# A list scheduler gets TensorE durations per pair of instructions, and puts a wide matmul between two fp32 transposes

## The chip, the cores and the metric

The kernel runs on one core of a Trainium2 chip. The metric is the device time of one execution in microseconds (us). The engines that matter are TensorE (PE in the profile; PEld is its weight load), VectorE (DVE), ScalarE (ACT), GpSimd (POOL) and SyncE (SP), whose queue issues the loads from memory.

## The reference

Two transformer blocks of two layers each run one after the other on 512 tokens of 1024 channels, all in fp32. Cut to what is computed:

```
# block 1
x = x + diff_attention(rms_norm(x))             # 8 heads, two causal softmaxes per head, a = p0 - lam * p1
x = x + swiglu(rms_norm(x))                     # hidden width 2816
x = x + swa_sink_attention(rms_norm(x))         # 16 query heads, 4 key heads, window 128, a sink per head
x = x + swiglu(rms_norm(x))
# block 2, with a second stream xc of 256 context tokens and shifts and gates from silu(c) @ w_mod
x  = x  + g1 * conv_mixers(modulate(rmsnorm(x)))     # depthwise convolutions of 3 and 31 taps
xc = xc + cg1 * conv_mixers(modulate(rmsnorm(xc)))
x, xc = each + gate * conv_ffn(modulate(rmsnorm(.))) # hidden width 2816, a convolution of 3 taps
x = x + g1 * windowed_gqa(x, xc)                     # 128-token blocks, three blocks and the context as keys
x = x + g2 * conv_ffn(modulate(rmsnorm(x)))
return rmsnorm(x, final_norm)
```

## The kernel before

Activations lie with channels on the 128 partitions and tokens along the free axis, so the stream is 8 tiles of 128 x 512. Every fp32 product is made of three products in float32r: a value is split into a rounded part and a remainder, and `mm3` (L727) issues high x high, high x low and low x high into the same PSUM bank. A product's stationary operand has 128 columns, its moving operand 512 or 256 (half of the tokens, or the context), 384 or 128 in the attentions.

Four other kinds of instruction run on PE. Their names in the profile's rows are the tiles that they read:

- an fp32 transpose of 128 x 128 (`psum_t<-arenaF`, 128x128). Attention transposes the softmax's weights, up to four blocks in a row (L1204 and L1585); `bcast` (L690) makes a column of one factor per token into a row for all partitions, as the last step of a norm; the end of the kernel turns its output (L1843). There are 566.
- a float32r transpose of 128 x 128 (`psum_t<-arenaR`, 128x128), four in a row per token block of queries and keys (L984). There are 296.
- an fp32 product with a single column of ones (`psum_t<-arenaF`, 128x1), which sums squares over the partitions (`colsum_rsqrt`, L677). There are 80, and the trace has two records for each.
- narrow float32r products of 128 columns, 112 of them, in rows like those of the float32r transposes.

A norm of a stage is a chain through three engines: the squares' sums (128x1) on PE, Ln and Exp on ScalarE, a Newton step on VectorE, `bcast` on PE, and then the scaled tiles on VectorE and ScalarE, which the next products read. Attention has a chain of its own for every block of queries: scores on PE, mask, maximum and exponential on VectorE and ScalarE, transposes on PE, the split on ScalarE and VectorE, then the products with the values.

**What sets the order.** The kernel's functions don't issue instructions: they record them. `Rec.add` (L275) notes for each its dependences and a cost in ns (`cost`, L314). When a stage is recorded, `issue` (L343) sets the order in seven rounds of list scheduling: `forward` (L393) gives each engine, whenever it is free, the ready instruction with the lowest priority number; `backward` (L455) runs the same from the end and returns for each instruction the latest start that does not lengthen the schedule, which is the priority number of the next round. The shortest of the schedules is issued, and so is fixed for every engine. A copy may go to ScalarE or VectorE (`flex`, L269), whichever the schedule finds free. The numbers for PE are per instruction:

```python
            if fn == "transpose":
                return 59 if dt == F32R else 109
            if dt == F32:
                return max(n * 1.685, 214)
            if dt == F32R:
                return max(n * 0.4222, 107)
```

so 216 ns for 512 columns and 108 for 256, and an engine is free again when the cost has passed. The functions that the diff touches follow.

Of the kernel before, what the change touches and what calls it, by code (L numbers as in the profile page):

```python
# [19 lines left out]
S = 512  # L20
# [12 lines left out]
ROUNDS = 7  # L33
WO1_AT = (2, 3, 5, 7)
# [20 lines left out]
# ---------------------------------------------------------------- column map of the parameter table  # L55
# [125 lines left out]
# ---------------------------------------------------------------- recorded program  # L181
# Instructions are recorded in program order and issued in an order that a list scheduler finds: every
# instruction stays behind those that it depends on (data, or reuse of the same on-chip memory).
# [4 lines left out]
# the activation functions whose tables are not in every set; ln and exp can be had together  # L188
# [12 lines left out]
class Rec:  # L201
    ENG = ("tensor", "vector", "scalar", "gpsimd", "sync")

    def __init__(self, nc, psum):
# [13 lines left out]
        self.free = {e: 0.0 for e in self.ENG}  # L218
        self.dma = 0.0
# [3 lines left out]
    # regions as keys  # L223
# [45 lines left out]
    def flex(self, first, second):  # L269
        """(engine, function, args, kwargs) twice: the same work on either engine, the first preferred"""  # L270
        eng, fn, a, k = second
        o, i = self.add(*first, flex=True)
        self.alt[len(self.ops) - 1] = (eng, fn, a, k, self.cost(eng, fn, a, k, o, i))

    def add(self, eng, fn, a, k, flex=False):  # L275
# [9 lines left out]
        for x in ins:  # L285
            for key in self.keys(x):
# [4 lines left out]
                if key[0] == "p":  # L291
                    # two engines never read a bank at the same time
# [11 lines left out]
        self.ops.append((eng, fn, a, k, deps, self.cost(eng, fn, a, k, outs, ins), i + self.bias))  # L304
        return outs, ins
# [8 lines left out]
    def cost(self, eng, fn, a, k, outs, ins):  # L314
# [3 lines left out]
        if eng == "tensor":  # L318
            dt = (k.get("rhs") if fn == "matmul" else a[1]).dtype
            if fn == "transpose":  # L320
                return 59 if dt == F32R else 109
            if dt == F32:
                return max(n * 1.685, 214)
            if dt == F32R:
                return max(n * 0.4222, 107)
            return max(n * 0.4222, 29)
# [16 lines left out]
    def issue(self, until=None):  # L343
        """order and issue what was recorded and not issued yet, or only as much as it takes to issue the set `until`"""
# [17 lines left out]
        # priorities: the order of the program at first, then the latest starts that leave the schedule as short as it is  # L362
# [13 lines left out]
        order, eng, fin, self.free, self.dma = self.forward(todo, succ, pred, at, prio, wanted)  # L376
# [12 lines left out]
    def lat(e, e2):  # L389
        """from the end of an instruction to the start of one that waits for it"""  # L390
        return (0 if e == "tensor" else 260) if e2 == "tensor" else (197 if e == "tensor" else 130)

    def forward(self, todo, succ, pred, at, prio, wanted=None):  # L393
# [1512 lines left out]
```

## Time and profile before

| | us |
|---|---|
| median of 3 runs (lowest to highest) | 2588.99 (2587.46 to 2589.8) |
| the profiled execution: span from the first to the last instruction, all that is recorded of its time | 2587.4 |
| PE busy | 2554.9 |
| VectorE busy | 1873.2 |
| ScalarE busy | 1252.5 |
| PE waiting for another engine, in gaps over 0.15 us | 25.6 |

In the profile a matmul's duration runs from its start to its modelled end, and several overlap; how far apart two starts are tells the pace. The timeline merges instructions that follow each other on one line with the same tiles into one row, which shows the start of the first, the time to the end of the last, the first one's shape and the count. A stretch that is cut to a few ns begins with the instruction that is then running, and so shows one instruction's start.

### The profile page before, as it was taken

Reading aid. Unit: us, or ns where it says so; the run is one execution under the profiler, and the core shown is the slowest. Engines: PE = TensorE matmul, PEld = TensorE weight load, DVE = VectorE, ACT = ScalarE, POOL = GpSimd, SP = SyncE. Lnnn points to the kernel's source line nnn. Section 1 sums busy time; section 2 is a strip of 40 time slices with the busy share of each in tenths; the row PEclk is TensorE's granted clock in tenths of the full one; section 3 lists DMA queues with packets and bytes.
Section 4 is the critical chain, followed back from the end, with each engine's and each line's share of the span. In section 5 each row is a group of like instructions: output and inputs, shape, how many; then the busy total and the mean of one; then the engine's idle time right before and its main releaser. Section 6 shows DMA issues by size and latency. Waiting matters only on the chain.

```text
span 2587.4 us, 38865 instructions
## 1 busy us (share of the span) xinstructions
PE 2554.9 (99%) x15122; PEld 2263.3 (87%) x15122; DVE 1873.2 (72%) x3499; ACT 1252.5 (48%) x2361; POOL 131.0 (5%) x252
## 2 busy tenths in 40 slices
PE   8999999999999999999999999999999999999998
PEld 8998988889979888889888988888889988888887
DVE  8888999845898999449986753454556899864555
ACT  6876522224896322336664431231335798532333
POOL 0000000000010000004830000000000000000000
PEclk9999999999999999999999999999999999999999
DMA  4122567632125676322122112122112111333332
GB/s 147 57 62 71 188 211 220 180 95 78 58 66 155 203 223 195 120 90 66 58 66 62 58 58 73 58 62 70 58 58 63 50 34 42 98 98 98 94 99 69
DMA packets 73337, 252.80 MB, mean 98 GB/s; under 512 B 8513, under 2 KB 10689, under 8 KB 72769
## 3 DMA queue, kind: packets, MB, share of 16 engines
q1 hardware_dynamic: 73152, 250.32, 31.9%
q8 instruction: 118, 1.93, 0.3%
q14 instruction: 67, 0.54, 0.1%
HBM read 248.19 MB, written 2.10 MB: 97 GB/s over the span
## 4 chain that ended last, share of the span: by engine, by line
PE 93%; DVE 3%; POOL 2%; ACT 2%; issue 1%; DMA 0%; DVEq 0%; POOLq 0%; SPq 0%; ACTq 0%
PE psum_t L384 93%; POOL arenaZ L384 2%; DVE arenaR L384 1%; DVE arenaF L384 1%; ACT arenaF L384 1%; ACT arenaR L384 1%; DMA arenaF<-in_wqkv_dram 0%; DMA arenaF<-in_xT_dram 0%; ACT L382 0%; ACT L384 0%; DVE psum_t L384 0%; ACT arenaZ L384 0%; DVEq L1902 0%; DVE arenaZ L384 0%; POOLq L384 0%
## 5 line engine op out<-in xcount | busy, mean ns | idle before, releaser
L384 PE MATMUL psum_t<-arenaR 128*128 128x256 f32 (+2 forms) x13304 | 2374.1, 337 | 13.1 <-ACT arenaR L384 7.9
L384 PEld LDWEIGHTS psum_t<-arenaR 128*128 128x128 f32 x13304 | 2050.0, 188 | 280.0 <-ACT arenaR L384 9.0
L384 ACT CAST arenaR<-arenaF 128x1024 fp32r<-128x1024 f32 (+4 forms) x500 | 447.9, 899 | 816.5 <-PE psum_t L384 622.5
L384 DVE TENSOR_TENSOR arenaR<-arenaF,arenaR 128x1024 fp32r<-128x1024 f32 (+3 forms) x508 | 529.4, 1049 | 154.2 <-ACT arenaR L384 150.5
L384 ACT ACTIVATE arenaF<-arenaF 128x256 f32<-128x256 f32 (+9 forms) x776 | 405.9, 542 | 236.5 <-DVE arenaF L384 201.1
L384 DVE SCALAR_TENSOR_TENSOR arenaF<-psum_t,arenaF 128x511 f32<-128x511 f32 (+5 forms) x416 | 262.7, 634 | 287.2 <-PE psum_t L384 163.5
L384 DVE CUSTOM_DVE_ANT_0 arenaF<-arenaF 128x1024 f32<-128x1024 f32 x192 | 246.0, 1281 | 10.0 <-DMA arenaF<-in_wmod_dram 4.6
L384 DVE TENSOR_TENSOR arenaF<-arenaF 128x512 f32<-128x512 f32 (+5 forms) x430 | 220.6, 525 | 27.6 <-ACT arenaF L384 21.8
L384 DVE TENSOR_TENSOR arenaF<-psum_t,arenaF 128x512 f32<-128x512 f32 (+1 forms) x236 | 142.5, 611 | 134.9 <-PE psum_t L384 133.9
L384 PE MATMUL psum_t<-arenaZ,arenaR 128*128 128x256 f32 (+3 forms) x1024 | 178.1, 304 | 2.3 <-DVE arenaF L384 1.4
L384 ACT CAST arenaR<-psum_t 128x512 fp32r<-128x512 f32 (+3 forms) x332 | 157.2, 480 | 28.7 <-PE psum_t L384 25.7
L384 ACT ACTIVATE arenaF<-psum_t,arenaF 128x512 f32<-128x512 f32 (+3 forms) x204 | 109.0, 548 | 111.4 <-PE psum_t L384 103.6
L384 PEld LDWEIGHTS psum_t<-arenaZ,arenaR 128*128 128x128 f32 x1024 | 145.5, 189 | 12.8 <-DVE arenaF L384 2.7
L384 POOL TENSOR_TENSOR arenaZ<-arenaZ,arenaF 128x256 f32<-128x256 f32 x120 | 104.3, 870 | 446.7 <-DVE arenaF L384 423.6
L384 PE MATMUL psum_t<-arenaF 128*128 128x128 f32 (+2 forms) x730 | 114.2, 268 | 9.5 <-DVE arenaF L384 4.1
L384 DVE CUSTOM_DVE_ANT_0 arenaF<-psum_t,arenaF 128x256 f32<-128x256 f32 (+3 forms) x208 | 103.8, 512 | 14.3 <-PE psum_t L384 13.2
L384 PEld LDWEIGHTS psum_t<-arenaF 128*128 128x128 f32 x730 | 89.5, 152 | 21.3 <-DVE arenaR L384 4.9
L384 DVE TENSOR_TENSOR arenaR<-psum_t,arenaR 128x512 fp32r<-128x512 f32 (+4 forms) x169 | 99.1, 591 | 12.2 <-ACT arenaR L384 10.8
L384 POOL COPY arenaF<-arenaF 128x1 f32<-128x1 f32 x128 | 26.5, 234 | 1599.1 <-DVE arenaF L384 1172.7
L384 ACT ACTIVATE arenaR<-arenaF 128x256 fp32r<-128x256 f32 (+1 forms) x168 | 81.7, 525 | 32.3 <-DVE arenaF L384 24.4
L384 DVE SCALAR_TENSOR_TENSOR arenaR<-arenaF,arenaR 128x256 fp32r<-128x256 f32 (+1 forms) x168 | 79.5, 505 | 8.0 <-ACT arenaR L384 7.7
L384 DVE SCALAR_TENSOR_TENSOR arenaF<-arenaF 128x256 f32<-128x256 f32 (+8 forms) x258 | 79.9, 332 | 3.5 <-ACT arenaF L384 1.9
(47 smaller groups left out, 450.2 us busy)
## 6 DMA issues: line engine op xcount, KB each, us to landing
arenaF<-in_wmod_dram SPq DMA_DIRECT2D x96, 512.0 KB, 4.3
arenaF<-in_wgu_dram SPq DMA_DIRECT2D x88, 512.0 KB, 3.8
arenaF<-in_wup_dram SPq DMA_DIRECT2D x88, 512.0 KB, 3.6
arenaF<-in_wqkv_dram SPq DMA_DIRECT2D x35, 512.0 KB, 3.7
arenaF<-in_wd_dram SPq DMA_DIRECT2D x32, 448.0 KB, 3.3
arenaF<-in_wdn_dram SPq DMA_DIRECT2D x32, 448.0 KB, 3.3
arenaF<-in_wab_dram SPq DMA_DIRECT2D x20, 512.0 KB, 3.6
arenaF<-in_wd_dram SPq DMA_DIRECT2D x16, 512.0 KB, 4.3
```

What stands on the lines that cost most here:

```text
L384: getattr(getattr(self.nc, e), fn)(*a, **k)
```

## The change

The scheduler's model of PE changes, and nothing that is computed. The costs of an instruction become n / 2.4 + 13.3 ns for float32r products (227 for 512 columns, 120 for 256), 85 for a float32r transpose, and at least 224 for an fp32 product. Each PE instruction gets a kind: F for fp32, S for float32r transposes and products under 256 columns, L for wide float32r products. How long one holds PE depends on the next (`hold`): an fp32 transpose 109 ns before another F, 28 ns before anything else; S before S 62 ns; all others their cost. Its result still comes after its cost. `forward` keeps a second heap, `between`, of the ready L instructions. Where the next instruction would be an F behind an F, the ready L of the lowest priority number is taken first, if its number is less than SLACK = 4000 ns above that of the F. `backward` uses 48 ns for an fp32 transpose and 62 for S. All comments and docstrings are taken out too, which shifts the line of the issuing call from L384 to L387.

```diff
+SLACK = 4000
...
+        self.kinds = {}
+        self.pe = None
...
+        if eng == "tensor":
+            self.kinds[i] = self.kind(i)
...
             if fn == "transpose":
-                return 59 if dt == F32R else 109
+                return 85 if dt == F32R else 109
             if dt == F32:
-                return max(n * 1.685, 214)
-            if dt == F32R:
-                return max(n * 0.4222, 107)
-            return max(n * 0.4222, 29)
+                return max(n * 2 / 1.2, 224)
+            return max(n / 2.4 + 13.3, 110)
...
+    def kind(self, i):
+        _, fn, a, k = self.ops[i][:4]
+        if (k.get("rhs") if fn == "matmul" else a[1]).dtype == F32:
+            return "F"
+        return "S" if fn == "transpose" or self.fsize(a[0]) < 256 else "L"
+
+    def hold(self, i, j):
+        fn, c = self.ops[i][1], self.ops[i][5]
+        x, y = self.kinds[i], self.kinds[j]
+        if x == "F" and fn == "transpose":
+            return 109 if y == "F" else 28
+        return 62 if x == y == "S" else c
...
     def forward(self, todo, succ, pred, at, prio, wanted=None):
...
+        between = []
...
                     heapq.heappush(ready[e], (prio[i] + (e != ops[i][0]) * 10000, i))
+                    if e == "tensor" and kinds[i] == "L":
+                        heapq.heappush(between, (prio[i], i))
             _, i = heapq.heappop(ready[e])
+            if e == "tensor":
+                while between and between[0][1] in took:
+                    heapq.heappop(between)
+                if kinds[i] == "F" and pe is not None and kinds[pe[0]] == "F" and between and between[0][0] < prio[i] + SLACK:
+                    heapq.heappush(ready[e], (prio[i], i))
+                    _, i = heapq.heappop(between)
+                if pe is not None:
+                    t = max(t, pe[1] + self.hold(pe[0], i))
+                pe = i, t
...
+            elif e == "tensor":
+                fin[i] = t + c
+                free[e] = t + (28 if kinds[i] == "F" else 62 if kinds[i] == "S" else c)
             else:
                 free[e] = fin[i] = t + c
...
     def backward(self, todo, succ, pred, took, fin):
...
+            elif e == "tensor":
+                done = t + c
+                free[e] = t + (48 if self.kinds[i] == "F" and ops[i][1] == "transpose" else 62 if self.kinds[i] == "S" else c)
```

The change moves instructions on PE nearly everywhere outside the feed-forward layers. Three places follow, each with PE's rows before and then now.

**Place A**, PE, a head of the first attention (the trace of before has it from 104.5 us on). `arenaF 128x128` are the four fp32 transposes of a query block's weights, `arenaR 128x256` and `128x384` products. Before:

```order
L384 MATMUL psum_t<-arenaF 128x128
L384 MATMUL psum_t<-arenaR 128x256 x12
L384 MATMUL psum_t<-arenaF 128x128 x4
L384 MATMUL psum_t<-arenaR 128x256 x8
L384 MATMUL psum_t<-arenaR 128x384 x2
```

Now:

```order
L387 MATMUL psum_t<-arenaR 128x384 x2
L387 MATMUL psum_t<-arenaR 128x256
L387 MATMUL psum_t<-arenaF 128x128
L387 MATMUL psum_t<-arenaR 128x256
L387 MATMUL psum_t<-arenaF 128x128
L387 MATMUL psum_t<-arenaR 128x256
L387 MATMUL psum_t<-arenaF 128x128
L387 MATMUL psum_t<-arenaR 128x256
L387 MATMUL psum_t<-arenaF 128x128
L387 MATMUL psum_t<-arenaR 128x256 x11
```

The same four transposes now have a product of 256 columns between each two of them.

**Place B**, PE, the same attention some 7 us earlier (98.5 us in the trace of before). `arenaR 128x128 x4` are the four float32r transposes of a block of queries and keys, `arenaF 128x128` fp32 transposes. Before:

```order
L384 MATMUL psum_t<-arenaR 128x256 x15
L384 MATMUL psum_t<-arenaF 128x128 x4
L384 MATMUL psum_t<-arenaR 128x256 x12
L384 MATMUL psum_t<-arenaR 128x128 x4
L384 MATMUL psum_t<-arenaR 128x256 x12
```

Now:

```order
L387 MATMUL psum_t<-arenaR 128x256 x10
L387 MATMUL psum_t<-arenaR 128x128
L387 MATMUL psum_t<-arenaR 128x256
L387 MATMUL psum_t<-arenaR 128x128
L387 MATMUL psum_t<-arenaR 128x256
L387 MATMUL psum_t<-arenaR 128x128
L387 MATMUL psum_t<-arenaR 128x256
L387 MATMUL psum_t<-arenaF 128x128
L387 MATMUL psum_t<-arenaR 128x128
L387 MATMUL psum_t<-arenaR 128x256
```

The four float32r transposes are taken apart too, by products and by an fp32 transpose.

**Place C**, PE, the end of the second block's attention (2198.9 us on in the trace of before), where a norm begins. `arenaF 128x1` are that norm's column sums, the last `arenaF 128x128 x2` before is its `bcast`, `arenaR,arenaZ 128x512` are products with the values. Before:

```order
L384 MATMUL psum_t<-arenaF 128x128 x4
L384 MATMUL psum_t<-arenaR,arenaZ_11793 128x512 x2
L384 MATMUL psum_t<-arenaR 128x512
L384 MATMUL psum_t<-arenaR 128x256 x2
L384 MATMUL psum_t<-arenaR 128x512 x2
L384 MATMUL psum_t<-arenaR 128x256 x4
L384 MATMUL psum_t<-arenaR 128x512
L384 MATMUL psum_t<-arenaR 128x256
L384 MATMUL psum_t<-arenaF 128x1 x2
L384 MATMUL psum_t<-arenaR 128x256 x18
L384 MATMUL psum_t<-arenaF 128x128 x2
L384 MATMUL psum_t<-arenaR 128x256 x130
```

Now:

```order
L387 MATMUL psum_t<-arenaF 128x128
L387 MATMUL psum_t<-arenaR,arenaZ_11792 128x512
L387 MATMUL psum_t<-arenaF 128x128 x5
L387 MATMUL psum_t<-arenaR 128x512
L387 MATMUL psum_t<-arenaF 128x1
L387 MATMUL psum_t<-arenaR 128x512
L387 MATMUL psum_t<-arenaF 128x1
L387 MATMUL psum_t<-arenaR 128x512 x2
L387 MATMUL psum_t<-arenaF 128x128
L387 MATMUL psum_t<-arenaR 128x256
L387 MATMUL psum_t<-arenaF 128x128
L387 MATMUL psum_t<-arenaR 128x256 x114
```

The 18 products that stood between the sums and the `bcast` now stand behind it; products that stood ahead of the sums stand between them.

## Rows read from the trace of the kernel before

**Rows 1.** The page's busy times with shares, and PE's granted clock by slices.

```profile
PE 2554.9 (99%) x15122; PEld 2263.3 (87%) x15122; DVE 1873.2 (72%) x3499; ACT 1252.5 (48%) x2361; POOL 131.0 (5%) x252
...
PEclk9999999999999999999999999999999999999999
```

**Rows 2.** The page's chain that ended last, share by engine.

```profile
PE 93%; DVE 3%; POOL 2%; ACT 2%; issue 1%; DMA 0%; DVEq 0%; POOLq 0%; SPq 0%; ACTq 0%
```

**Rows 3.** PE's waits by releaser: us in total, times, longest.

```profile
PE psum_t L384 <- ACT arenaR L384: 7.9, 4, 6.5
PE psum_t L384 <- DVE arenaR L384: 7.7, 12, 1.8
PE psum_t L384 <- DVE arenaF L384: 7.2, 10, 2.4
PE psum_t L384 <- ACT arenaZ L384: 2.5, 2, 1.6
PE psum_t L384 <- ACT arenaF L384: 0.3, 1, 0.3
```

**Rows 4.** PE's timeline, two long runs: start us, us, line, operation, shape, xcount.

```profile
309.81 30.54 PE L384 MATMUL psum_t<-arenaR 128*128 128x512 f32 x134
...
29.84 10.36 PE L384 MATMUL psum_t<-arenaR 128*128 128x256 f32 x85
```

**Rows 5.** PE's timeline around place A, cut to show single starts.

```profile
104.50 0.27 PE L384 MATMUL psum_t<-arenaF 128*128 128x128 f32 x1
104.53 1.68 PE L384 MATMUL psum_t<-arenaR 128*128 128x256 f32 x12
...
105.92 0.28 PE L384 MATMUL psum_t<-arenaR 128*128 128x256 f32 x1
...
106.04 0.60 PE L384 MATMUL psum_t<-arenaF 128*128 128x128 f32 x4
106.39 2.25 PE L384 MATMUL psum_t<-arenaR 128*128 128x256 f32 x16
...
106.60 0.40 PE L384 MATMUL psum_t<-arenaR 128*128 128x256 f32 x2
```

**Rows 6.** PE's timeline, fp32 transposes among products of 512 columns.

```profile
2138.03 0.60 PE L384 MATMUL psum_t<-arenaF 128*128 128x128 f32 x4
...
2138.70 0.27 PE L384 MATMUL psum_t<-arenaF 128*128 128x128 f32 x1
2138.73 0.94 PE L384 MATMUL psum_t<-arenaR 128*128 128x512 f32 x3
...
2139.04 0.39 PE L384 MATMUL psum_t<-arenaR 128*128 128x512 f32 x1
```

**Rows 7.** PE's timeline, float32r transposes: four at place B, one elsewhere.

```profile
98.48 0.45 PE L384 MATMUL psum_t<-arenaR 128*128 128x128 f32 x4
...
98.97 0.40 PE L384 MATMUL psum_t<-arenaR 128*128 128x256 f32 x2
...
664.93 0.39 PE L384 MATMUL psum_t<-arenaR 128*128 128x128 f32 x2
...
665.16 0.40 PE L384 MATMUL psum_t<-arenaR 128*128 128x256 f32 x2
```

**Rows 8.** PE's timeline at a norm; in brackets idle before, and releaser.

```profile
1956.35 0.61 PE L384 MATMUL psum_t<-arenaF 128*128 128x1 f32 x4
1956.82 1.91 PE L384 MATMUL psum_t<-arenaR 128*128 128x256 f32 x14
1959.66 0.43 PE L384 MATMUL psum_t<-arenaF 128*128 128x128 f32 x2 [0.93 <-DVE arenaF L384]
```

**Rows 9.** PE's timeline, stalls in block 2's attention and at place C.

```profile
2111.54 0.66 PE L384 MATMUL psum_t<-arenaF 128*128 128x128 f32 x4 [1.85 <-DVE arenaR L384]
...
2204.22 1.45 PE L384 MATMUL psum_t<-arenaR 128*128 128x256 f32 x10 [1.25 <-DVE arenaR L384]
2206.20 0.38 PE L384 MATMUL psum_t<-arenaR 128*128 128x256 f32 x1 [0.54 <-DVE arenaF L384]
```

More of the change, by code (lines that the diff above doesn't have):

```diff
@@ L375, in issue @@
                 prio = best[1]
-        order, eng, fin, self.free, self.dma = self.forward(todo, succ, pred, at, prio, wanted)
+        order, eng, fin, self.free, self.dma, self.pe = self.forward(todo, succ, pred, at, prio, wanted)
         for i in order:
@@ L391, in lat @@
         return (0 if e == "tensor" else 260) if e2 == "tensor" else (197 if e == "tensor" else 130)
+    def kind(self, i):
[9 more added lines that the diff above has]
+        return 62 if x == y == "S" else c
     def forward(self, todo, succ, pred, at, prio, wanted=None):
-        ops, alt, lat = self.ops, self.alt, self.lat
-        free, dma = dict(self.free), self.dma
+        ops, alt, lat, kinds = self.ops, self.alt, self.lat, self.kinds
+        free, dma, pe = dict(self.free), self.dma, self.pe
+        between = []
         left = {i: len(pred[i]) for i in todo}
@@ L452, in forward @@
                     push(s)
-        return order, took, fin, free, dma
+        return order, took, fin, free, dma, pe
     def backward(self, todo, succ, pred, took, fin):
```

## The prediction

> **What bounds the kernel now.** I read the page's busy line and clock line first: the reader is to see TensorE (PE) busy for 99% of the span, VectorE 72%, ScalarE 48%, and a clock line with no slice below nine tenths [rows 1]. Then the chain of work that ended last: 93% of it is PE's own instructions following each other [rows 2]. Then PE's waits by releaser: 25.6 us in all (7.9 + 7.7 + 7.2 + 2.5 + 0.3) [rows 3]. The longest of them, 6.5 us, is the wait for the first operands, which no reordering touches, so 19.1 us of stalls are left. Everything else is the pace at which PE starts one instruction after the other. So the change can act in two ways only: through that pace, and through those 19.1 us. DMA ends none of PE's waits [rows 3], so the moved issues on SP's queue cost nothing; what hides them is that the weights wait in their buffers.
>
> A matmul's listed duration is pipelined and says little about pace, so I read starts. 134 products of 512 columns last from 309.81 to 340.35 [rows 4], and a lone one at 2139.04 is 0.39 long [rows 6]: (30.54 - 0.39) / 133 = 0.227 us from start to start. 85 of 256 columns take 10.36 us [rows 4], one at 105.92 is 0.28 long [rows 5]: (10.36 - 0.28) / 84 = 0.120 us.
>
> **The premise: 28 ns after a transpose.** The new table says that an fp32 transpose holds PE 109 ns before another fp32 instruction, but 28 ns before a wide product. Both numbers stand in the trace. Four transposes start at 106.04 and the product behind them at 106.39: 0.35 = 3 x 0.109 + 0.028. A single one starts at 104.50, its product at 104.53 [rows 5]. But the next row has the bill. After the four, the first product of 256 columns holds PE from 106.39 to 106.60, 0.20 us in place of 0.120. So four transposes cost 106.60 - 106.04 - 0.12 = 0.44 us, 0.11 each. The single one: from 104.50 to 106.04 there are one transpose and 12 products; 1.54 - 12 x 0.120 = 0.10 us. A transpose costs 0.10 to 0.11 us whether it stands alone or in four: 81 ns saved at its own start are lost in the following product. Beside products of 512 columns it is the same: four and their product take 2138.70 - 2138.03 = 0.67, less 0.227 leaves 0.44, 0.11 each; a single one and its product 2139.04 - 2138.70 = 0.34 us against 0.109 + 0.227 = 0.336 [rows 6].
>
> The Trainium skill speaks against the change here: "TensorE: Matmul & The Clock Gate", section "LDWEIGHTS (loading the stationary operand)", has a load take its columns divided by 1.2, 107 ns for 128, so a short transpose cannot cover the load of what follows it. The rows agree: 0.028 + 0.08 makes 0.108. By that rule the transposes' term is 0; by the new table it is -24.8 us, the first rival below. The same page, section "The mechanism", lets a load overlap running matmuls only where they use other rows of the array. Here all use all 128, and that would put 0.107 us ahead of every product; the row of 85 products has 0.120 us for load and product together, so loads do hide behind a product and the measurement decides. By that section interleaving would be free everywhere, 0 for the next term too; the sum would then be 4.1 us less.
>
> **The change part by part.** The same 15,040 PE instructions are issued; counted in the two orders, neighbours of two fp32 transposes fall from 384 to 78, so 306 are split.
>
> - fp32 transposes before 256 columns (160 of the 306): 0, by the price above. Before 512 (96): 4 ns each, 0.4 us. The other 50 stand before products of 384 or 128 columns or float32r transposes, taken as 0. Bounds: 0 to 2 us.
> - float32r transposes. The new rule is only about fp32, but products pulled forward also land between these: runs rise from 80 to 257 (place B). Four in a row start at 98.48, the second product behind them at 98.97: 0.49 - 0.12 = 0.37 us. One alone starts at 664.93, the second product behind it at 665.16: 0.23 - 0.12 = 0.11 us [rows 7]. So each added run costs (4 x 0.11 - 0.37) / 3 = 0.023 us more: 177 x 0.023 = 4.1 us. A hundredth either way in the starts gives the bounds: 0.10 alone makes 0.01, 0.12 alone 0.037, so 2 and 7 us; 0 if the delay of the product is absorbed where it stands before 512 columns.
> - fp32 column sums of one column: 49 neighbours fall to 0, and none stands alone in the trace. Two take 1956.82 - 1956.35 = 0.47 us [rows 8]. If alone they cost what a transpose does, 0.11 in place of 0.235, it is -6 us; if they pay the float32r step, +1 us. I take 0: two passes mean two loads, which the nearest row prices alike in any company.
> - 20 copies move from ScalarE to VectorE (the scheduler's own choice), 33 in place of 13. VectorE is busy 72% of the span [rows 1], so some 0.6 us each lies beside PE's work, and costs only where PE waits for VectorE, which is in the next term.
> - Stalls. In the model PE now runs through transposes 81 ns too fast, and the rule takes products early that used to stand where PE waits for a chain. Place C shows it: the column sums of a norm are followed in the old order by 18 products before the norm's broadcast, in the new one by two of 512, 0.45 us. What that chain takes is seen at another norm, where PE did wait for it: from 1956.82, behind the sums, to the broadcast at 1959.66, 2.84 us [rows 8]. So PE idles some 2.84 - 0.45 = 2.4 us there, where it now idles 1.25 + 0.54 = 1.79 [rows 9]: +0.6 us. Queued behind the waiting broadcast are the 114 products that would have covered it, and the rest of the norm on VectorE waits for it. Over the whole program I counted, at the paces above, the PE work between the last PE instruction that a wait goes back to and the instruction that waits: under 1.0 us in 26 places before, in 52 now. If stalls followed that count they would double, +19 us; on the other side, ahead of the transposes that now wait 1.85 us at 2111.54 [rows 9] the same count gives 3.2 us of work in place of 1.4, and if half of today's stalls dissolved in that way it would be -10 us. I take +5, a quarter of the doubling, since most of the short covers sit in the same few places, where one wait absorbs the next.
>
> Sum: 0.4 + 4.1 + 0 + 5 = 9.5 us on the profiled execution's 2587.4: 2596.9. The runs' median of 2588.99 lies 1.6 above that execution, so 2598.5; I say 2598. Its own range, with the pace at 0 to 9 and the stalls at 0 to 10: 2589 to 2608.
>
> **Rivals.**
> 1. The 28 ns are real wherever transpose and product alternate: 306 x 0.081 = 24.8 us gained, less the 4.1: 2589 - 20.7 = 2568. For it: the starts behind the transposes [rows 5]. Against it: the start after the next in the same rows, and the single transpose among products of 512 columns [rows 6]. Chance 0.04.
> 2. Not slower, by fewer stalls: the table's wide products are now 120 and 227 ns, as the trace has them [rows 4], where the old formula gave 108 and 216, so the planner sees how long PE covers a chain and places consumers later. The place is the two grouped-query attentions, with stalls like that at 2111.54 [rows 9]. Its price is up to half of 19.1: 2589 + 4.5 - 10 = 2583.5. It decides for faster once stalls fall by 9.7 us, and against it stands the count of short covers. Chance 0.12, half of it beyond that point.
> 3. The stalls come out as they were, and only the pace shows: 2589 + 4.5 = 2593.5. Chance 0.19.
> 4. The short covers bite one by one, stalls double: 2589 + 4.5 + 19 = 2612.5. Chance 0.15.
>
> **How the numbers follow.** The forecast has the remaining 0.50. What a measurement of this kernel can tell from no change is about 0.2%, 5.2 us. Faster: rival 1 and half of rival 2, 0.10. Within: the other half and rival 3 without a little, 0.24. Slower: the forecast, rival 4 and that little, 0.66. The range reaches down to 2585, nearly to rival 2, and up to 2613, rival 4; the column sums' -6 is inside it unless it joins with fewer stalls.
>
> **What would show it.** In the new trace a product of 256 columns behind a lone transpose should hold PE 0.20 us, one of 512 some 0.31, so that no alternating stretch is shorter than before. A lone float32r transpose should cost 0.11 to 0.12 us with its product's delay. PE's waits should sum to about 31 us with the first, place C some 2.4 us of it. I am wrong on the pace if the product behind a lone transpose keeps to 0.120 or 0.227 us; I am wrong on the stalls if the waits sum to 20 us or less.

## The result and the profile after

The changed kernel takes 2610.85 us (median of 4, 2609.57 to 2615.04), the kernel before beside it 2588.22 (2587.18 to 2589.8). The ratio is 1.009, 95% interval 1.0075 to 1.0104: slower by 22.6 us, where I forecast 9. It lies inside the range on record and outside the likeliest case's own range.

From here on all times in rows, spans and splits are those of the profiled executions. That of the changed kernel has a span of 2613.2 us and is the longest of its four (the others 2607.8 to 2609.2); before it was 2587.4. The page's busy line, clock line and chain, which answer to [rows 1, 2]:

```profile
PE 2574.9 (99%) x15122; PEld 2272.9 (87%) x15122; DVE 1878.1 (72%) x3520; ACT 1242.1 (48%) x2340; POOL 133.3 (5%) x252
...
PEclk9999999999999999999999999999999999999999
...
PE 89%; DVE 5%; ACT 3%; POOL 1%; issue 1%; DMA 1%; DVEq 0%; POOLq 0%; SPq 0%; ACTq 0%
```

PE is as busy as before, its own share of the chain falls from 93% to 89%, VectorE's and ScalarE's rise: PE waits more. PE's waits by releaser (us in total, times, longest), against [rows 3]:

```profile
PE psum_t L387 <- DVE arenaR L387: 10.9, 15, 2.2
PE psum_t L387 <- ACT arenaR L387: 9.5, 9, 6.4
PE psum_t L387 <- DVE arenaF L387: 6.8, 10, 1.3
PE psum_t L387 <- ACT arenaZ L387: 2.3, 1, 2.3
PE psum_t L387 <- ACT arenaF L387: 1.0, 3, 0.5
```

They sum to 30.5, forecast 31. But that view lists only what leaves PE visibly idle, in gaps over 0.15 us. A wait can show at the weight load of the instruction alone, and the rows of PEld list more of them. Before:

```profile
PEld psum_t L384 <- DVE arenaR L384: 11.4, 16, 2.3
PEld psum_t L384 <- DVE arenaF L384: 10.0, 14, 2.5
PEld psum_t L384 <- ACT arenaR L384: 9.0, 5, 6.5
PEld psum_t L384 <- issue: 3.6, 7, 2.1
PEld psum_t L384 <- ACT arenaF L384: 2.6, 7, 0.7
PEld psum_t L384 <- ACT arenaZ L384: 1.1, 1, 1.1
```

And now:

```profile
PEld psum_t L387 <- DVE arenaR L387: 14.8, 25, 2.6
PEld psum_t L387 <- ACT arenaR L387: 13.1, 15, 6.4
PEld psum_t L387 <- DVE arenaF L387: 10.9, 18, 1.5
PEld psum_t L387 <- ACT arenaF L387: 5.6, 9, 2.4
PEld psum_t L387 <- ACT arenaZ L387: 3.1, 3, 2.5
PEld psum_t L387 <- issue: 1.5, 6, 0.5
```

37.7 us in 50 waits have become 49.0 in 76: +11.3, where PE's rows show +4.9 (25.6 in 29 and 30.5 in 38). The rows named "issue", for which the view shows no releaser, are in both sums; without them it is 34.1 in 43 and 47.5 in 70. Of the 11.3, 8.5 lie between 1960 and 2240 us (9.8 before, 18.3 now), in block 2's attention. There is place C (timeline of PE; idle time before and its releaser in brackets):

```profile
2224.28 0.38 PE L387 MATMUL psum_t<-arenaF 128*128 128x1 f32 x2 [0.22 <-DVE arenaR L387]
...
2226.29 0.32 PE L387 MATMUL psum_t<-arenaF 128*128 128x128 f32 x1 [0.60 <-DVE arenaF L387]
...
2228.34 1.01 PE L387 MATMUL psum_t<-arenaR 128*128 128x256 f32 x3 [1.20 <-DVE arenaR L387]
```

0.22 + 0.60 + 1.20 = 2.02 us of PE's idle time, 1.79 before [rows 9], 2.4 forecast. But the forecast put its 2.4 ahead of the norm's broadcast (the transpose at 2226.29), where PE idles 0.60; the 1.20 is the wait of the products behind it. What the forecast did not have at all comes next. Busy time by stretches (us, then busy us and instructions of PE, PEld, DVE, ACT and POOL, granted clock, DMA share, GB/s), in the changed kernel:

```profile
230.50:240.70 10.20, 9.34 (x39) 8.47 (x39) 8.04 (x24) 7.13 (x18) 0.00 (x0) 0.50 0.01 2
...
1268.40:1271.60 3.20, 0.94 (x5) 0.76 (x5) 2.11 (x4) 2.38 (x6) 2.89 (x5) 1.00 0.01 5
1271.60:1275.00 3.40, 3.40 (x10) 2.63 (x9) 3.40 (x8) 3.09 (x7) 2.69 (x5) 0.50 0.00 0
...
1971.30:1974.70 3.40, 3.40 (x19) 3.40 (x18) 0.90 (x6) 1.35 (x3) 0.00 (x0) 0.50 0.04 14
...
2196.60:2200.00 3.40, 3.36 (x11) 2.19 (x10) 2.94 (x7) 2.62 (x4) 0.18 (x1) 0.50 0.37 122
...
2227.30:2234.10 6.80, 5.76 (x27) 5.76 (x28) 5.93 (x14) 3.49 (x8) 0.00 (x0) 0.50 0.00 1
```

and before:

```profile
228.00:231.40 3.40, 3.27 (x12) 2.62 (x13) 3.40 (x9) 0.81 (x3) 0.00 (x0) 0.50 0.00 0
...
2112.20:2115.60 3.40, 2.88 (x10) 2.50 (x11) 3.30 (x9) 2.48 (x5) 0.00 (x0) 0.51 0.26 100
```

Each of these stretches but the second row runs at 1.2 GHz (granted clock 0.50), and each begins behind a stall of PE or in one (the second row is the stall ahead of 1271.6: PE busy 0.94 of 3.20 us). There were 6.8 us of them, now there are 27.2. In a clock line of 65 us per slice none of it shows.

**Where the 25.8 us between the two spans went.** I split each profiled execution in the same way. Pace: for every PE instruction outside the half-clock stretches, the median distance to the next start over all kernels of this study, by the shapes of the instruction and its two neighbours; summed, this is what the order costs with no wait. Half clock: what the starts inside those stretches exceed these medians by. Stalls: the rest of the span (with the start and the end, which are nearly the same in all), so errors of the other two land here. Taking the medians in other ways, for rare neighbours above all, moves the differences between kernels by about 1 us.

| kernel | median us | ratio, 95% interval | span | pace | stalls | half clock: excess (us at half) | loads' waits, "issue" included (times) |
|---|---|---|---|---|---|---|---|
| before | 2588.22 | | 2587.4 | 2537.6 | 46.9 | 2.9 (6.8) | 37.7 (50) |
| after | 2610.85 | 1.009 [1.0075, 1.0104] | 2613.2 | 2542.8 | 58.6 | 11.8 (27.2) | 49.0 (76) |
| e1 no rule | 2609.67 | 1.0083 [1.0068, 1.0098] | 2607.8 | 2542.3 | 59.2 | 6.3 (13.6) | 50.4 (74) |
| e2 rule only | 2599.02 | 1.0043 [1.0028, 1.0058] | 2598.0 | 2538.7 | 50.1 | 9.2 (20.4) | 44.9 (75) |
| e3 costs only | 2597.76 | 1.0037 [1.0024, 1.005] | 2595.9 | 2537.8 | 53.1 | 5.0 (10.2) | 48.4 (96) |
| e4 true holds | 2602.49 | 1.0058 [1.0041, 1.0074] | 2600.3 | 2538.1 | 54.5 | 7.7 (17.0) | 49.2 (89) |
| e5 float32r kept | 2602.54 | 1.0057 [1.0042, 1.0072] | 2600.7 | 2538.8 | 56.5 | 5.4 (10.2) | 47.7 (73) |
| e6 five rounds | 2586.86 | 0.9997 [0.9987, 1.0006] | 2584.3 | 2537.6 | 46.7 | 0 | 37.6 (51) |
| e7 latency 600 | 2599.85 | 1.005 [1.0035, 1.0065] | 2598.4 | 2537.5 | 51.4 | 9.5 (20.4) | 45.2 (62) |
| e8 holds, 500 | 2596.52 | 1.0038 [1.0024, 1.0052] | 2593.1 | 2538.2 | 52.1 | 2.8 (6.8) | 44.2 (83) |
| e9 filled stalls | 2609.97 | 1.0086 [1.0071, 1.0101] | 2608.4 | 2549.2 | 56.3 | 2.9 (6.8) | 44.5 (73) |
| e10 wide true | 2600.08 | 1.0045 [1.0031, 1.006] | 2598.6 | 2537.6 | 56.1 | 4.9 (10.2) | 47.8 (82) |
| e11 wide 0.40 | 2600.28 | 1.0048 [1.0031, 1.0065] | 2598.5 | 2538.0 | 54.0 | 6.5 (13.6) | 46.9 (78) |
| e12 wide 0.4214 | 2590.69 | 1.001 [1.0001, 1.0019] | 2586.4 | 2537.6 | 48.8 | 0 | 39.3 (55) |

So the changed kernel has +5.2 us of pace, +11.7 of stalls and +8.9 of half clock. The half clock differs between executions of one kernel: the mean granted clock of the profiled one is 0.994, of the other three 0.995, 0.995 and 0.996, so the 8.9 is on the high side for this kernel. The ratios go by runs of the kernel before beside each (2587.45 to 2588.53). A load's wait is not lost in full, since the product ahead of it may still be running; the stalls' column has what is lost. By the distances between starts, about half of the added stalls (some 6 us) stand where PE's rows show a wait, about a third (some 3.5 us, at 32 starts against 14) where only the load's row shows one with a releaser, and the rest at neither.

### The profile page after: what moved, and what is told of

Its sections match the earlier page's. It is cut to its first block, busy times and chain, and to the rows that moved or that the text cites. A ratio compares the mean times of both kernels' runs of the same rounds, so it can differ in the third digit from the quotient of the medians.

```text
span 2613.2 us, 38862 instructions
## 1 busy us (share of the span) xinstructions
PE 2574.9 (99%) x15122; PEld 2272.9 (87%) x15122; DVE 1878.1 (72%) x3520; ACT 1242.1 (48%) x2340; POOL 133.3 (5%) x252
## 3 DMA queue, kind: packets, MB, share of 16 engines
q1 hardware_dynamic: 73152, 250.32, 30.5%
## 4 chain that ended last, share of the span: by engine, by line
PE 89%; DVE 5%; ACT 3%; POOL 1%; issue 1%; DMA 1%; DVEq 0%; POOLq 0%; SPq 0%; ACTq 0%
PE psum_t L387 89%; DVE arenaF L387 2%; DVE arenaR L387 2%; POOL arenaZ L387 1%; ACT arenaF L387 1%; ACT arenaR L387 1%; DVE psum_t L387 1%; ACT arenaZ L387 0%; DMA arenaF<-in_wqkv_dram 0%; DMA arenaF<-in_wmod_dram 0%; DMA arenaF<-in_wgu_dram 0%; ACT L387 0%; DMA arenaF<-in_xT_dram 0%; ACT L385 0%; ACT psum_t L387 0%
## 5 line engine op out<-in xcount | busy, mean ns | idle before, releaser
L387 PE MATMUL psum_t<-arenaR 128*128 128x256 f32 (+3 forms) x13304 | 2421.5, 340 | 20.8 <-ACT arenaR L387 9.1
L387 PEld LDWEIGHTS psum_t<-arenaR 128*128 128x128 f32 (+1 forms) x13304 | 2076.2, 189 | 299.1 <-ACT arenaR L387 12.2
L387 ACT CAST arenaR<-arenaF 128x1024 fp32r<-128x1024 f32 (+4 forms) x483 | 437.6, 911 | 789.5 <-PE psum_t L387 567.0
L387 DVE TENSOR_TENSOR arenaR<-arenaF,arenaR 128x1024 fp32r<-128x1024 f32 (+3 forms) x508 | 527.2, 1044 | 156.2 <-ACT arenaR L387 153.0
L387 ACT ACTIVATE arenaF<-arenaF 128x256 f32<-128x256 f32 (+9 forms) x775 | 403.4, 539 | 294.4 <-DVE arenaF L387 257.0
L387 DVE SCALAR_TENSOR_TENSOR arenaF<-psum_t,arenaF 128x511 f32<-128x511 f32 (+5 forms) x416 | 262.9, 634 | 286.8 <-PE psum_t L387 165.1
L387 DVE CUSTOM_DVE_ANT_0 arenaF<-arenaF 128x1024 f32<-128x1024 f32 x192 | 245.9, 1281 | 8.2 <-DMA arenaF<-in_wmod_dram 3.1
L387 DVE TENSOR_TENSOR arenaF<-psum_t,arenaF 128x512 f32<-128x512 f32 (+1 forms) x236 | 142.4, 610 | 144.6 <-PE psum_t L387 144.0
L387 DVE TENSOR_TENSOR arenaF<-arenaF 128x512 f32<-128x512 f32 (+4 forms) x430 | 220.2, 524 | 30.6 <-ACT arenaF L387 24.4
L387 PE MATMUL psum_t<-arenaZ,arenaR 128*128 128x256 f32 (+3 forms) x1024 | 182.5, 308 | 0.6 <-DVE arenaF L387 0.4
L387 ACT CAST arenaR<-psum_t 128x512 fp32r<-128x512 f32 (+3 forms) x330 | 155.9, 480 | 32.8 <-PE psum_t L387 29.6
L387 PE MATMUL psum_t<-arenaF 128*128 128x128 f32 (+2 forms) x730 | 161.7, 264 | 6.9 <-DVE arenaF L387 4.7
L387 ACT ACTIVATE arenaF<-psum_t,arenaF 128x512 f32<-128x512 f32 (+3 forms) x204 | 108.8, 545 | 114.3 <-PE psum_t L387 102.7
L387 PEld LDWEIGHTS psum_t<-arenaZ,arenaR 128*128 128x128 f32 x1024 | 146.3, 189 | 12.0 <-DVE arenaF L387 1.7
L387 POOL TENSOR_TENSOR arenaZ<-arenaZ,arenaF 128x256 f32<-128x256 f32 x120 | 103.2, 862 | 439.7 <-ACT arenaF L387 430.8
L387 PEld LDWEIGHTS psum_t<-arenaF 128*128 128x128 f32 x730 | 103.5, 152 | 16.5 <-DVE arenaF L387 6.1
L387 DVE CUSTOM_DVE_ANT_0 arenaF<-psum_t,arenaF 128x256 f32<-128x256 f32 (+3 forms) x208 | 103.8, 511 | 16.7 <-PE psum_t L387 14.9
L387 POOL COPY arenaF<-arenaF 128x1 f32<-128x1 f32 x128 | 29.9, 250 | 1627.7 <-DVE arenaF L387 1185.0
L387 DVE TENSOR_TENSOR arenaR<-psum_t,arenaR 128x512 fp32r<-128x512 f32 (+4 forms) x169 | 98.7, 590 | 14.1 <-ACT arenaR L387 12.5
L387 ACT ACTIVATE arenaR<-arenaF 128x256 fp32r<-128x256 f32 (+1 forms) x168 | 81.2, 522 | 35.0 <-DVE arenaF L387 29.4
L387 DVE SCALAR_TENSOR_TENSOR arenaR<-arenaF,arenaR 128x256 fp32r<-128x256 f32 (+1 forms) x168 | 79.7, 505 | 12.2 <-ACT arenaR L387 12.0
L387 DVE SCALAR_TENSOR_TENSOR psum_t<-arenaF,psum_t 128x512 f32<-128x512 f32 x120 | 82.5, 746 | 1.1 <-ACT psum_t L387 0.9
```

Source lines behind the costliest of these rows:

```text
L387: getattr(getattr(self.nc, e), fn)(*a, **k)
```

## The experiments

### Which part of the change it is (e1 to e4)

e1, the changed kernel without the rule that puts a wide product between:

```diff
-SLACK = 4000
+SLACK = -1e12
```

> The changed kernel without the rule that puts a product between two fp32 transposes (SLACK so low that it never applies); the new costs and the pair durations stay. In its order 120 fp32 neighbours are left (384 before, 78 changed) and the float32r transposes stand in 257 runs, as in the changed kernel. Theory A, the model's pair durations (28 and 62 ns) thin out PE's cover and the rule adds little: pace +4, stalls and clock nearly as in the changed kernel, 2603 to 2611. Theory B, the rule alone eats the products that cover the chains: only the pace is left, 2590 to 2595. Theory C, the 28 ns are a gain and the rule's gain is hidden by stalls: slower than the changed kernel, over 2612.

2609.67 us, no measurable difference from the changed kernel. Fp32 neighbours are 120 (of 384), runs of float32r transposes 257 as with the rule: the costs and holds alone take both apart.

e2, the kernel before with the rule alone, old costs, no holds:

```diff
+                if kinds[i] == "F" and pe is not None and kinds[pe] == "F" and between and between[0][0] < prio[i] + SLACK:
+                    heapq.heappush(ready[e], (prio[i], i))
+                    _, i = heapq.heappop(between)
```

> The kernel before with its old costs, and only the rule (a wide product between two fp32 transposes, SLACK 4000). 98 fp32 neighbours are left, the float32r transposes stay in 83 runs. All theories of no gain from 28 ns: the pace is that of before within 2 us, since a lone fp32 transpose costs 0.11 us like one of four. Theory A: stalls hardly grow, 2588 to 2596. Theory B: stalls and half clock of the changed kernel, 2604 to 2612. Theory C: 25 us less pace, 2570 to 2580.

2599.02 us. Fp32 neighbours fall to 98 and the float32r runs stay at 83, and the pace rises by 1.1 us only, where 28 ns per split would have gained over 20: splitting fp32 transposes is nearly free and gains nothing. The rest of the loss is stalls (+3.2, the loads' waits +7.2) and half clock (+6.3).

e3, the kernel before with the new costs alone:

```diff
-                return 59 if dt == F32R else 109
+                return 85 if dt == F32R else 109
-                return max(n * 1.685, 214)
+                return max(n * 2 / 1.2, 224)
-                return max(n * 0.4222, 107)
+            return max(n / 2.4 + 13.3, 110)
```

> The kernel before with only the new costs per instruction (227 and 120 ns for products of 512 and 256 columns, 85 for a float32r transpose, 224 for fp32 products); no pair durations, no rule. Transposes stay grouped (384 neighbours, 77 runs). If the wide products' truer numbers help, fewer stalls: 2578 to 2586. If they are worth nothing, 2586 to 2593. If a new order alone scatters by as much as the change did, anything up to 2605.

2597.76 us, with numbers that are nearer to the trace. Pace as before, stalls +6.2, loads' waits +10.7, in 96 waits; PE's own rows sum to 25.5 us, as before (25.6). An example, PE's timeline, first merged and then cut to show single starts:

```profile
65.88 6.08 PE L382 MATMUL psum_t<-arenaR 128*128 128x256 f32 x47
...
67.74 0.28 PE L382 MATMUL psum_t<-arenaR 128*128 128x256 f32 x1
...
68.06 0.39 PE L382 MATMUL psum_t<-arenaR 128*128 128x256 f32 x1
...
68.28 0.40 PE L382 MATMUL psum_t<-arenaR 128*128 128x256 f32 x2
```

and the loads in the same stretch:

```profile
65.85 1.96 PEld L382 LDWEIGHTS psum_t<-arenaR 128*128 128x128 f32 x17
68.06 2.03 PEld L382 LDWEIGHTS psum_t<-arenaR 128*128 128x128 f32 x15 [0.25 <-ACT arenaR L382]
```

PE's merged row has no wait, yet two products of 256 columns in it take 0.32 and 0.22 us to the next start, 0.30 more than 2 x 0.120. The load's row has the cause, 0.25 us behind ScalarE.

e4, the changed kernel without the rule and with the holds as the trace has them:

```diff
-            return 109 if y == "F" else 28
-        return 62 if x == y == "S" else c
+            return 109
+        return 90 if x == y == "S" else max(c, 110)
```

(and 109 and 90 in place of 28, 48 and 62 where `forward` and `backward` set the engine free).

> The changed kernel with pair durations as the starts two instructions on show them: an fp32 transpose holds PE 109 ns before anything, a short float32r instruction 90 ns, or 110 before a wide one; no rule. 375 fp32 neighbours, 88 runs of float32r transposes, few short covers (as before). Theory A and B both: the pace of before, stalls of before or less, 2580 to 2592. If the extra half clock and stalls came from the new costs of the wide products, 2600 or more.

2602.49 us. The float32r runs are whole again (88) and the pace is that of before, +0.5; the stalls (+7.6) and the half clock (+4.8) stay. So most of the stalls do not need the 81 ns that the change believes in: the true hold has +7.6 of them, the costs alone (e3) +6.2, the changed kernel +11.7.

### The pace term by itself (e5)

```diff
-        return 62 if x == y == "S" else c
+        return c
```

(and `c` in place of 62 in `forward` and `backward`).

> The changed kernel, but the planner no longer lets a second float32r transpose or narrow product start 62 ns after the first; each holds PE for its own cost (85 or 110 ns). Runs of float32r transposes fall from 257 to 84 in the order, fp32 neighbours stay split (82 left of 384). Theory (the split float32r transposes are the pace term): the pace of PE falls by some 4 us to that of the run with the rule alone, and with stalls and half-clock stretches as in the changed kernel the time is 2606 to 2608 us. Rival (a split costs nothing, the pace comes from the fp32 transposes): the pace stays, 2610 to 2612 us. A second rival, that any other order draws its own stalls: the pace falls all the same, but the time lands anywhere from 2595 to 2615.

2602.54 us. The pace falls by 4.0 us, from 2542.8 to 2538.8: the price of 173 split runs, 0.023 us each, forecast 4.1 for 177. (With the medians taken in other ways the fall is up to 5.5 us, 0.032 each, so the close match is partly luck; it stays within the forecast's bounds.) The time falls by 8.3 in the median, more than the theory expected: with the other order 2.1 us of stalls and 6.4 of half clock went too, as the second rival had it. What splits them is the 62 ns after which the planner lets the next narrow one start, not the rule.

### Is it the order as such? (e6, e10, e11, e12)

e6 changes nothing that the planner knows:

```diff
-ROUNDS = 7
+ROUNDS = 5
```

> The kernel before, with five rounds of the planner in place of seven: the same costs, the same rules, only another order of the same quality by the planner's own measure. Fp32 neighbours 382 (384), float32r runs 78 (80), short covers 31 (26), so by the pace nothing changes. Theory (stalls follow the short covers): 2588 to 2592 us. Rival (the order before is a favourable draw, and any other order costs stalls and half-clock stretches): 2595 to 2602 us, as the run with the costs alone gave.

2586.86 us, the same as before, below what either theory expected. But 97% of PE's neighbours are kept, so it is a weak test. e10 and e11 move the wide products' cost to the true one and to the other side:

```diff
-                return max(n * 0.4222, 107)
+            return max(n / 2.4 + 13.3, 110)      # e10
+                return max(n * 0.40, 102)         # e11
```

> The kernel before, with one part of the new cost table alone: a wide product costs its columns / 2.4 + 13.3 ns (120 and 227) in place of 0.4222 per column (108 and 216); fp32 and the float32r transposes' costs as before. The weight loads' waits were 37.7 us in 50 waits in the kernel before and 48.4 in 96 with the whole cost table. Theory (the planner's too cheap products were its cover: with the true price it leaves fewer of them over each chain): loads wait 45 us or more, 2594 to 2599 us. Rival (it was the other costs, a float32r transpose at 85 in place of 59, or an fp32 product at 224): loads wait 36 to 40 us, 2586 to 2590 us.

> The kernel before, with its wide products made cheaper still: 0.40 ns per column (102 and 205 ns) in place of 0.4222. Theory (too cheap products are cover): the planner puts more of them over each chain, loads wait 30 to 37 us, 2580 to 2587 us. Rival (short covers, counted in the order at the measured paces, set the stalls): they rise from 26 to 55, so loads wait 45 us or more, 2594 to 2602 us. Second rival (any move of the costs away from the old ones costs some 10 us, whichever way): also 2594 to 2602 us, and the wide products' true price alone the same.

2600.08 and 2600.28 us, loads' waits 47.8 and 46.9: the theory that cheap products give cover falls with e11, which made them cheaper still. Both directions lose 12 us. e12 asks whether any other order does:

```diff
-                return max(n * 0.4222, 107)
+                return max(n * 0.4214, 107)
```

> The kernel before, with the planner's cost of a wide product at 0.4214 ns per column in place of 0.4222: 0.2% of it, 0.2 ns for 256 columns, which says nothing new of the engine. Yet the order comes out otherwise: 3668 of the 15,040 PE instructions stand at another place and 90% of the neighbours are kept (97% with five rounds, 88% with the true costs, 82% in the changed kernel). Theory (the order before is a favourable draw, and what the other edits lost beside their pace they lost by leaving it): 2594 to 2602 us, loads wait 44 to 49 us. Rival (what the planner is told of the costs is what counts, and so small an edit tells it nothing): 2586 to 2591 us, loads wait 36 to 40 us.

2590.69 us, 1.001 [1.0001, 1.0019]: a tenth of a per cent, with a quarter of the PE instructions moved. That speaks against the theory of the favourable draw but does not end it: 90% of the neighbours are kept here, 82% in the changed kernel, so the orders near the one before may be good together. Loads' waits by cost per 256 columns are 46.9 us (102 ns), 39.3 (107.9), 37.7 (108.1) and 47.8 (120): a dip at the cost that stood there. What makes it a dip these runs do not show.

### More cover (e7, e8)

```diff
-        return (0 if e == "tensor" else 260) if e2 == "tensor" else ...
+        return (0 if e == "tensor" else 600) if e2 == "tensor" else ...   # e7; 500 in e8, upon e4
```

> The kernel before, but the planner takes 600 ns in place of 260 from the end of another engine's instruction to the start of the PE instruction that waits for it, so it leaves more PE work over each chain: short covers 23 (26), their missing cover summed to 1.5 us each is 32.1 us (40.5). Theory (stalls follow the short covers): 3 to 6 us fewer stalls, 2582 to 2586 us. Rival (the order before is a favourable draw): 2595 to 2602 us.

> The run with the true holds (an fp32 transpose 109 ns whatever follows, no rule), and the planner takes 500 ns in place of 260 from another engine's end to PE's start. Short covers 14 (26 before, 35 with the true holds alone), their missing cover 25.4 us (40.5 and 40.9). Theory (stalls follow the short covers): stalls fall by 6 to 10 us against the kernel before, 2578 to 2583 us. Rival (the order before is a favourable draw): 2595 to 2605 us, as the true holds alone.

2599.85 and 2596.52 us: the rival's times, loads' waits 45.2 and 44.2. So my count of short covers does not set the stalls: 23 and 14 of them here (26 before) went with longer waits, 55 in e11 with about the same. e8 against e4 gains 5.0 us of waits, so the longer latency helps the true holds, not the order before.

### The half clock (e9)

44 products that nobody reads, with the operands of the last wide product, are put ahead of five instructions for which PE idles, in the order of the changed kernel; the table has the PE instruction's number, a PSUM bank that is free there, and how many (together 6.4 us of pace):

```diff
+FILL = {1686: (6, 8), 11415: (3, 9), 13007: (4, 16), 13185: (4, 2), 13189: (3, 9)}
...
+                    for _ in range(m):
+                        self.nc.tensor.matmul(self.psum[:, bank * 512:bank * 512 + w], lhsT=lhsT, rhs=rhs, start=True, stop=True)
```

> The changed kernel in its own order, with 44 products more on PE that nobody reads, put just ahead of five instructions before which PE idles: 8 of 512 columns at the stall that ends at 228.84 us, 9 of 256 at 1970.03, 16 of 256 at 2196.05, 2 of 512 at 2226.29 and 9 of 256 at 2228.34. By the paces 0.227 and 0.120 us each block is 0.1 to 0.3 us shorter than the idle time it stands in, so the stalls themselves stay. Theory (PE's own idle time brings the stretches at the granted clock of 1.2 GHz): the four stretches behind these places (10.2, 3.4, 3.4 and 6.8 us) are gone, the one at 1271.6 us, whose stall is left as it was, stays; 2599 to 2603 us against 2610.85. Rival (the half clock comes from something else, and the idle time before it is a coincidence): the five stretches stay, 2610 to 2612 us.

The stretches, at the places of the changed kernel's list (some 0 to 4 us earlier here):

```profile
233.70:237.10 3.40, 3.40 (x15) 3.30 (x16) 2.30 (x10) 2.28 (x7) 0.00 (x0) 0.50 0.01 2
1266.00:1269.40 3.40, 1.08 (x7) 0.83 (x7) 2.31 (x4) 2.40 (x5) 3.09 (x5) 1.00 0.04 16
1269.40:1274.00 4.60, 4.60 (x21) 3.78 (x21) 4.60 (x10) 4.20 (x9) 3.75 (x6) 1.00 0.00 0
...
1970.00:1974.00 4.00, 4.00 (x36) 4.00 (x35) 1.89 (x6) 1.11 (x3) 0.00 (x0) 1.00 0.02 4
...
2194.00:2198.00 4.00, 3.61 (x24) 3.01 (x25) 4.00 (x12) 4.00 (x9) 0.67 (x4) 1.00 0.47 131
...
2223.70:2227.10 3.40, 3.40 (x18) 3.40 (x17) 1.63 (x4) 1.67 (x4) 0.00 (x0) 0.50 0.00 0
```

Where the filler stood in the stall (1970, 2194) the half clock is gone: 36 PE instructions in 4.00 us, where 19 took 3.40. At 230 the 10.2 us are 3.4, behind shorter stalls that no filler covered. At 2223 the filler waited itself, and the half clock is there (PE's timeline; L396 is the filler, L400 the rest):

```profile
1278.31 1.88 PE L400 MATMUL psum_t<-arenaR 128*128 128x512 f32 x7 [0.81 <-ACT arenaZ L400]
...
2194.21 0.50 PE L400 MATMUL psum_t<-arenaR 128*128 128x512 f32 x1 [0.58 <-DVE arenaR L400]
...
2222.57 0.73 PE L396 MATMUL psum_t<-arenaR 128*128 128x512 f32 x2 [1.90 <-ACT arenaR L400]
```

The rival (the five stretches stay) is out, and the theory holds at the two places where the stall was really filled. It is not shown beyond that: at 1269 no filler stood, the stall is as long as before (PE busy 1.08 of 3.40 us), and the clock stays at 1.00 all the same, against the theory. So idle time of PE is not enough to bring the half clock, and at one of the five places the stretch went without being filled.

And the time hardly moves: 2609.97 against 2610.85, 4.8 us between the profiled spans. In the table the fillers add 6.4 us of pace; had they only filled idle time, the stalls would be 6.4 us less, but they are 2.3 less. So of the 8.9 us of excess taken away 4.1 came back as new stalls. The rows above show 2.7 of them: stalls of 0.81 and 0.58 us that the changed kernel did not have, in stretches that now run at 1.00, where PE comes too early, and 1.3 us more at 2222.57, which the filler itself brought. The Trainium skill, "TensorE: Matmul & The Clock Gate", section "Terms", puts the penalty at about the throttled time times one minus the clock's ratio; worked out from that page, 20.4 x 0.5 = 10.2 us is the estimate here. The starts agree in the stretch (8.9), the end of the program does not: 1 to 5 us came back. Executions of one kernel go the same way: of e2's four, the one with a mean granted clock of 0.998 took 2596.75 us and the two with 0.995 took 2599.48 and 2599.82, 3 us for what is, by an estimate from these clocks (0.003 x 2599 / 0.5), some 16 us at the half clock.

## Why the prediction was right and where it was not

**The bound** was read rightly as far as the engine goes: PE's starts set the end, and no wait on DMA appeared among PE's. That the change could act "in two ways only", by pace and by waits, was wrong: PE's clock is a third.

**The 28 ns.** Right. In the changed kernel's timeline transpose and product alternate:

```profile
2204.29 0.27 PE L387 MATMUL psum_t<-arenaF 128*128 128x128 f32 x1
2204.32 0.36 PE L387 MATMUL psum_t<-arenaR 128*128 128x256 f32 x1
2204.52 0.27 PE L387 MATMUL psum_t<-arenaF 128*128 128x128 f32 x1
...
2207.45 0.27 PE L387 MATMUL psum_t<-arenaF 128*128 128x128 f32 x1
2207.48 0.48 PE L387 MATMUL psum_t<-arenaR,arenaZ 128*128 128x512 f32 x1
2207.79 0.27 PE L387 MATMUL psum_t<-arenaF 128*128 128x128 f32 x1
```

0.03 and then 0.20 behind 256 columns, 0.03 and 0.31 behind 512, as forecast: the transpose's saving is paid back at once. Rival 1 is out.

**The float32r transposes.** The price was right, its reason not. A lone one (PE's timeline, cut to show single starts):

```profile
43.69 0.39 PE L387 MATMUL psum_t<-arenaR 128*128 128x128 f32 x2
...
43.75 0.34 PE L387 MATMUL psum_t<-arenaR 128*128 128x256 f32 x1
...
43.92 0.39 PE L387 MATMUL psum_t<-arenaR 128*128 128x128 f32 x2
```

Transpose and product take 0.23 us, 0.11 over the product's 0.120. I gave as the reason that products pulled forward land between them; e1 has 257 runs without the rule and e2 83 with it. It is the planner's 62 ns (e5). The pace came out at +5.2, forecast 4.5.

**Column sums and copies.** Right at 0. A lone column sum (two records) and its product, in the changed kernel's timeline:

```profile
98.88 0.28 PE L387 MATMUL psum_t<-arenaF 128*128 128x1 f32 x2
99.02 0.36 PE L387 MATMUL psum_t<-arenaR 128*128 128x256 f32 x1
99.22 0.28 PE L387 MATMUL psum_t<-arenaF 128*128 128x1 f32 x2
```

0.34 - 0.12 = 0.22 us with its product's delay; in company it was 0.235 before without that delay [rows 8], so standing alone saves nothing of note. VectorE has 21 more instructions (3520); whether any of PE's longer waits for VectorE comes from them these runs do not show.

**Stalls: the term that was mis-sized.** I took +5 and it was +11.7. The sum of PE's waits came out as forecast (30.5 for 31), but by luck, since my way to scale them, the count of short covers, does not govern them (e7, e8, e11). Place C's 2.02 for 2.4 is luck too: the chain from the sums to the broadcast took 2226.29 - 2224.98 = 1.31 us there, not the 2.84 of the other norm, and the longest wait, 1.20, came behind the broadcast. What failed is that I read stalls from PE's waits alone: the loads' rows, which I had not read, list many more, short ones that leave little or no idle time in PE's, and +4.9 us of PE's waits went with +11.7 of stalls. Nor is there one culprit: rule, costs and holds alone bring +7.2, +10.7 and, with the costs, +12.7 us of loads' waits, and all of it +11.3.

**The clock: a term that was missing.** 8.9 us by the starts inside the stretches. I saw a clock line without a slice below nine tenths, took the clock for constant, and so put this term at nothing. The stretch behind the stall at 2111.54 [rows 9] was in the trace of before, at 0.51. By e9 less than that would come back if it were gone, so part of it is not a cost of its own but hides stalls.

**The rivals.** Rival 4's time, 2612.5, is the nearest, but not its mechanism: the stalls did not double, and its count does not govern them. Rivals 2 and 3 (fewer stalls, the same stalls) are out by +11.7 us of stalls. That the range held is luck as well: it reached up to 2613 for rival 4's doubled stalls, and what filled it was a smaller rise of the stalls and a clock term that no part of the forecast had.

No kernel here beats the one before beyond the measurement.

## What to carry to other kernels

Price an instruction to the second start behind it: a start that comes early may be paid for in the next. Read an engine's stalls from what waits first, here the weight loads, not only from the engine's visible idle time, and look at the clock in windows of a few us behind every long stall. Numbers nearer to the truth need not give a better order: in this list scheduler they gave a worse one (e3, e4, e10), and so did a step the other way (e11). Why is not shown. So any such edit needs an edit of the same size the other way beside it before its result is laid to the truth of the numbers.

## What was not expected of the hardware

In the kernels before and after, the granted clock fell to 0.50 behind idle times of PE of 1.2 to 2.4 us, for 3.4 to 10.2 us, and did not fall at others: in the kernel before, PE was idle 1.64 us ahead of 1323.38 us and the stretch from 1321.7 to 1325.1 has 1.00. Nor does a longer idle time decide it. Where the kernel before idles 2.35 us and then falls (at 228.0), e12 idles 2.93 us and does not (PE's timeline, then the stretch behind it):

```profile
227.97 0.55 PE L384 MATMUL psum_t<-arenaF 128*128 128x128 f32 x3 [2.93 <-DVE arenaF L384]
...
228.00:231.40 3.40, 3.29 (x21) 2.65 (x21) 3.40 (x8) 1.83 (x5) 0.00 (x0) 1.00 0.00 0
```

What tells the two apart stays open. In a program that waits on other engines as often as this one, time at the half clock is partly cover: taking 20.4 us of it away gave back 1 to 5.
